# Hybrid diffusion layer: one 512-column matmul for the high and low activation parts, output blocks of 512 columns

## The chip, the cores and the metric

The kernel runs on one core of one Trainium2 chip. The metric is the device time of one execution in microseconds; the median of three runs of the kernel before is 2029.83 us (2029.54 to 2030.59).

## The reference

One layer of a backbone is applied to 128 context tokens and 128 latent tokens with the same weights, 2048 channels wide, all in float32. For each of the two rows of tokens:

```python
h = rmsnorm(x, norm1_g) * (1 + scale1) + shift1          # shift, scale, gate from silu(c) @ w_mod
parts = split(h @ w_in)                                  # 17440 columns
o_a = hgrn2_branch(...)                                  # gated linear recurrence, both directions
o_b = chunk_mlp_branch(...)                              # 128x128 mixing per channel group
o_c = gdn_branch(...)                                    # short conv, gated delta rule, both directions
merged = g_a * (o_a @ w_br_hg) + g_b * (o_b @ w_br_cm) + g_c * (o_c @ w_br_gdn)
x = x + gate1 * (merged @ w_out)
h2 = rmsnorm(x, norm2_g) * (1 + scale2) + shift2
x = x + gate2 * (square(relu(h2 @ w_ff1)) @ w_ff2)       # hidden width 8192
y = rmsnorm(x, final_g)
```

The outputs are y of both rows and the final states of the two recurrences of the context row.

## The kernel before

**The weight stream.** Activations lie channel-major, 128 channels on the partitions and 256 columns (128 context tokens, 128 latent tokens). Every weight matrix passes through SBUF once, in units of 128x1024 numbers (512 KB). ScalarE rounds a unit to float32r (`wh`, the high part) and VectorE subtracts (`wl`, the low part); `split` does it, three pairs of buffers ahead at most, and a split waits until TensorE has finished with the pair that it overwrites. The activations are split the same way into a high tile (`Hh`, `oah`, half of `hid`) and a low tile (`Hl`, `oal`, the other half). `block` multiplies: for each 128x128 weight block there are three matmuls with 256 moving columns each, high*high, low*high, high*low, all into the same 256 columns of PSUM:

```python
ops = ((hi[:, w], ah), (lo[:, w], ah), (hi[:, w], al))
```

I call these three a triple. The weight is the stationary operand and is loaded for each. A block is 1024 output columns (8 column tiles) wide; two column tiles share a PSUM bank of 512 numbers, so a block fills 4 of the 6 banks that the stream has. The loop goes over the k-tiles outside and the column tiles inside, so the first bank of a finished block is complete some 18 matmuls ahead of the last. When the block is done, `evac` empties its banks: one ScalarE or VectorE instruction per bank (activation function, product with a gate, residual, or copy). The next block starts in the two spare banks and then needs the first two banks of the block before.

Two blocks (`win(0)` and `win(10)`, orient "A") have it the other way around: the activations are stationary and 512 weight columns move. The last columns of `w_out` and `w_ff2` go in narrower blocks (`PIECES`).

**The fillers.** All mixer work (recurrences, conv, norms, the gMLP) is written as generators that `pump` interleaves with the stream's matmuls. A planner (`Clock`, `Meter`) computes when each engine gets to its instructions; `pump` adds filler stages while VectorE and ScalarE are at most `margin` (1.8 us) ahead of TensorE, and near a block's end at most `DVEE` = 2.0 us (VectorE) and `ACTE` = 0 (ScalarE) beyond the end that it expects. The planner takes 0.1093 us for a 256-column matmul. The lowest filler is the background, `mods`: it forms the modulation vectors gate1, shift2, scale2 and gate2 on VectorE (the tiles `junk<-mraw,cb`); `drain_mod` forces what is left of it where it is needed, ahead of `w_out` and of the second norm. `finish` emits all that is left of a filler, whatever TensorE has to wait for.

**One such place matters here.** `start_gmlp` (line 1498) starts the gMLP as a filler once its input `vBf` (slot 6) is there. The next block is `gate(1, 0, 6)`, whose result goes into slot 6 as well, so its `evac` first calls `self.finish(*self.before.values())` (line 1455): the gMLP must be done with `vB` by then. The gMLP consists of `head_rms`, four `part`s (two loads, four matmuls, three VectorE instructions each, with two scratch tiles between them, so two parts at a time) and four `parts` that split the result.

**Order of the stream.** Start (modulation columns, hff, half of hfb), hq, rest of hfb, hi, hgo, q, k, v, ggo, then gates and branch products in turn, `w_out`, second norm, and the MLP in four groups of 2048 hidden channels: `ff1` (relu, square, split) and `ff2` (partial sums in `Y`, at the end the residual `resid`).

Of the kernel before, what the change touches and what calls it, by code (L numbers as in the profile page):

```python
# [30 lines left out]
HEADS = 8  # L31
W = "wait"
# [9 lines left out]
class Clock:  # L42
    """A model of when every engine gets to its instructions: in order, each once the data and
    buffers that it names are free. The fillers are placed by it."""
# [11 lines left out]
    def place(self, tile, key, bufs):  # L56
        """A new tile in a pool's ring of buffers waits for the last use of the one before."""
# [34 lines left out]
    def book(self, e, reads, writes, cost, hop=0.0):  # L92
        """Start and end of an instruction of engine e."""
# [23 lines left out]
class Meter:  # L117
    """An engine whose instructions go into the clock."""
# [4 lines left out]
    def cost(self, name, a, k, out):  # L123
# [49 lines left out]
class Pool:  # L173
    """A tile pool whose tiles the clock knows."""
# [18 lines left out]
class Backbone:  # L193
    """Activations are channel-major ([channel, row*128 + token], row 0 the context, row 1 the
    latents). A weight matrix streams through SBUF once; each 128x128 block of it is the stationary
    operand of three float32r products (high*high, low*high, high*low), which together carry
    float32's mantissa."""
# [27 lines left out]
    def slot(self, z, shape, dt=F32):  # L225
# [7 lines left out]
        return v  # L233

# [47 lines left out]
    def grab(self):  # L282
        """A filler bank for work outside the fillers."""
# [33 lines left out]
    def step(self, g, forced=False):  # L317
        """One stage of a filler, once what its last stage did is ready; True if it did something."""
# [15 lines left out]
    def force(self, gens):  # L334
        """The stage that is ready first, of these fillers or else of any."""
# [6 lines left out]
    def finish(self, *gens):  # L342
        """Emit what is left of these fillers."""
# [6 lines left out]
    def together(self, *gens):  # L350
        """Runs generators side by side."""
# [5 lines left out]
    def now(self, gen):  # L357
        """Emit a generator at once; its value."""
# [8 lines left out]
    def rsqrt(self, v, n, tag, scale=None):  # L367
        """1/sqrt(v), with a Newton step after the square root and the reciprocal."""
# [13 lines left out]
    def split(self, hi, lo, x):  # L382
        """hi + lo == x exactly: hi rounds to float32r, lo is what is left."""
# [12 lines left out]
        # while the slots are empty they lend buffers to the start  # L396
# [53 lines left out]

    def block(self, units, nk, xh, xl, evac, orient="B", pre=None):
        """Steps of one block of output columns: NB columns a k-tile, or, where a unit holds two
        k-tiles, NB/2."""
# [4 lines left out]
        nb = 4 // per  # L458

        def do(u, hi, lo):  # L460
# [4 lines left out]
            if u >= len(units) - 2:  # L465
                self.evac = self.t["pe"] + 24 * 0.107 * (len(units) - u)
            for k in range(u * per, u * per + per):
                off = (k - u * per) * (NB // per)
                ah, al = xh(k), xl(k)
                for c in range(2 * nb if orient == "B" else nb):  # L470
                    if orient == "B":
                        o = st["b"][c // 2][:, (c % 2) * 256:(c % 2) * 256 + 256]
                        w = slice(off + c * P, off + c * P + P)
                        ops = ((hi[:, w], ah), (lo[:, w], ah), (hi[:, w], al))
                        first, lastc = c % 2 == 0, c % 2 == 1
                    else:
                        o = st["b"][c]
                        w = slice((c % 2) * 512, (c % 2) * 512 + 512)
                        t = slice((c // 2) * P, (c // 2) * P + P)
                        ops = ((ah[:, t], hi[:, w]), (ah[:, t], lo[:, w]), (al[:, t], hi[:, w]))  # L480
                        first = lastc = True
                    for j, (a, b) in enumerate(ops):
                        nc.tensor.matmul(o, lhsT=a, rhs=b, start=(k == 0 and j == 0 and first),
                                         stop=(k == nk - 1 and j == 2 and lastc), skip_group_check=True)
                    if lastc:
                        self.pump()
# [9 lines left out]
    def setup(self):  # L496
# [12 lines left out]
        # conditioning vectors: silu, then high and low parts as stationary columns  # L509
# [51 lines left out]
    def rstd(self, x, gain=None):  # L561
        """1/rms of every token, on all partitions, in a filler bank; the last two tiles go in here."""
# [25 lines left out]
    def modulate(self, which, n0, x, r, wait=True):  # L588
        """(x * r) * gs + shift for channel tiles n0, n0 + 1, split into the stream's operands."""
# [35 lines left out]
    def start_steps(self, first, second):  # L625
        """shift1 and scale1, 256 channels at a time, the input norm for those channels, and the
        products of the first blocks of input columns with them."""
# [11 lines left out]
        def bounds():  # L639
            # softmax over the one layer, minus its first entry  # L640
# [61 lines left out]
        for db in range(8):  # L702
            wins.append([dict(kind="call", do=lambda db=db: self.finish(self.chains[db])), first[2 * db]])
            wins += [[first[2 * db + 1]], [second[db]]]
# [1051 lines left out]
```

## Time and profile before

| | |
|---|---|
| median of three timed runs | 2029.83 us |
| span of the profiled execution | 2026.0 us |
| VectorE busy | 1492.9 us |
| ScalarE busy | 1016.9 us |
| mean granted TensorE clock | 0.994 |

The span runs from the first to the last instruction of the one profiled execution; the timed runs have 3.8 us more around it. All tensor instructions carry line 169, since one helper issues them, so groups are told apart by tiles: `pb` is a PSUM bank of the stream, `pf` one of the fillers, `z` any of the twelve slots, `wh` and `wl` the split weights. A row of the timeline gives the start, the length, the engine, the operation with out<-in, and how many instructions it merges; a start-to-start distance of neighbouring matmuls is what one costs, since their recorded lengths overlap. DVE is VectorE, ACT ScalarE, PE TensorE.

### The profile page before, as it was taken

The numbers are of one execution on the slowest core, as the hardware profiler recorded it, in microseconds if no ns is written. First come the engines' busy times: TensorE is split into PE (matmuls) and PEld (weight loads), VectorE is DVE, ScalarE is ACT, GpSimd is POOL, SyncE is SP. The second block draws the span as 40 slices with busy tenths as digits, with TensorE's granted clock in tenths as the row PEclk, the third lists the DMA queues.
The fourth block names the chain that finished last, engine by engine and source line by source line (L and its number), as shares of the span: only waits on it lengthen the run. The fifth ranks groups of instructions, "written<-read, shape, count | busy, mean of one in ns | idle before, by whom it ended". The sixth has DMA issues, their size and how long they took to land.

```text
span 2026.0 us, 39412 instructions
## 1 busy us (share of the span) xinstructions
PE 1980.4 (98%) x15829; PEld 1915.5 (95%) x15829; DVE 1492.9 (74%) x2662; ACT 1016.9 (50%) x1475; POOL 47.4 (2%) x117
## 2 busy tenths in 40 slices
PE   5999999999999999999999999899999999999997
PEld 3779989999999999899999999899999999999997
DVE  5886797967877997877888878588878554455565
ACT  6774645466645545365634434644444443344343
POOL 0000000000000001110000000000000000000000
PEclk9999999999999999999999999999999999999998
DMA  9887756665566767776778787577787555555654
GB/s 342 309 305 226 231 192 199 198 194 173 166 192 217 255 220 227 248 236 227 234 258 273 260 279 245 178 240 260 246 271 255 186 182 183 186 180 186 213 192 137
DMA packets 143055, 455.82 MB, mean 225 GB/s; under 512 B 16248, under 2 KB 16920, under 8 KB 141848
## 3 DMA queue, kind: packets, MB, share of 16 engines
q1 hardware_dynamic: 135216, 423.96, 63.4%
q0 software_dynamic: 7360, 29.07, 4.4%
q8 instruction: 124, 2.03, 0.4%
q14 instruction: 59, 0.48, 0.1%
q10 hardware_dynamic: 296, 0.27, 0.0%
HBM read 442.74 MB, written 10.50 MB: 224 GB/s over the span
## 4 chain that ended last, share of the span: by engine, by line
PE 90%; DVE 3%; DMA 3%; ACT 2%; issue 1%; SPq 0%; POOL 0%; DVEq 0%; ACTq 0%; POOLq 0%
PE pb L169 81%; PE pf L169 9%; DVE wl L169 1%; DVE z L169 1%; DVE m L169 1%; ACT wh L169 1%; DMA raw<-in_wmods 1%; DMA raw<-in_wouta 1%; DMA mraw<-in_wmodr 0%; DVE junk L169 0%; DMA z<-sp 0%; ACT tp L169 0%; DMA raw<-in_winh 0%; DMA raw<-in_win 0%; DMA z<-in_wmods 0%
## 5 line engine op out<-in xcount | busy, mean ns | idle before, releaser
L169 DVE TENSOR_TENSOR wl<-raw,wh 128x1024 fp32r<-128x1024 f32 x610 | 742.5, 1220 | 455.2 <-ACT wh L169 454.0
L169 ACT CAST wh<-raw 128x1024 fp32r<-128x1024 f32 x610 | 637.0, 1046 | 856.1 <-PE pb L169 745.2
L169 PE MATMUL pb<-Hh,wh 128*128 128x256 f32 x3144 | 898.5, 286 | 4.0 <-ACT Hh L169 2.6
L169 PE MATMUL pb<-Hl,wh 128*128 128x256 f32 x3144 | 890.5, 283 | 2.2 <-DVE Hl L169 2.2
L169 PE MATMUL pb<-Hh,wl 128*128 128x256 f32 x3144 | 890.3, 283 | 0.9 <-DVE wl L169 0.8
L169 PEld LDWEIGHTS pb<-Hh,wh 128*128 128x128 f32 x3144 | 602.4, 192 | 8.0 <-ACT Hh L169 3.0
L169 PEld LDWEIGHTS pb<-Hl,wh 128*128 128x128 f32 x3144 | 602.2, 192 | 3.1 <-DVE Hl L169 3.0
L169 PEld LDWEIGHTS pb<-Hh,wl 128*128 128x128 f32 x3144 | 602.5, 192 | 2.2 <-DVE wl L169 1.3
L169 PE MATMUL pb<-z,wh 128*128 128x256 f32 x2816 | 508.5, 283 | 0.0
L169 PEld LDWEIGHTS pb<-z,wh 128*128 128x128 f32 x2816 | 437.3, 190 | 0.2 <-DVE z L169 0.2
L169 PE MATMUL pb<-z,wl 128*128 128x256 f32 x1408 | 397.4, 282 | 0.0
L169 DVE SCALAR_TENSOR_TENSOR junk<-mraw,cb 128x512 bf16<-128x512 f32 x512 | 330.7, 685 | 16.4 <-DMA mraw<-in_wmodr 14.1
L169 PEld LDWEIGHTS pb<-z,wl 128*128 128x128 f32 x1408 | 268.2, 190 | 0.2
L169 DVE TENSOR_TENSOR z<-z,z 128x512 fp32r<-128x512 f32 (+2 forms) x76 | 59.1, 823 | 7.3 <-ACT z L169 7.2
L169 DVE SCALAR_TENSOR_TENSOR cy<-z,par,cy 128x258 f32<-128x258 f32 (+1 forms) x192 | 53.6, 331 | 1.9
L169 PE MATMUL pb<-wh,Hh 128*128 128x512 f32 x128 | 53.4, 417 | 0.0
L169 PE MATMUL pf<-m,z 128*128 128x128 f32 x384 | 50.5, 275 | 0.4 <-DVE m L169 0.4
L169 ACT ACTIVATE z<-pb 128x512 f32<-128x512 f32 x88 | 48.5, 600 | 3.5 <-PE pb L169 0.5
L169 PE MATMUL pb<-wh,Hl 128*128 128x512 f32 x128 | 50.1, 391 | 0.0
L169 PE MATMUL pb<-wl,Hh 128*128 128x512 f32 x128 | 50.0, 390 | 0.0
L169 PEld LDWEIGHTS pf<-m,z 128*128 128x128 f32 x384 | 47.6, 192 | 2.1 <-DVE m L169 1.0
L169 ACT CAST z<-z 128x512 fp32r<-128x512 f32 (+1 forms) x56 | 40.2, 771 | 17.7 <-PE pb L169 9.0
(171 smaller groups left out, 1323.2 us busy)
## 6 DMA issues: line engine op xcount, KB each, us to landing
raw<-in_win SPq DMA_DIRECT2D x249, 512.0 KB, 4.0
raw<-in_wff SPq DMA_DIRECT2D x224, 512.0 KB, 3.9
mraw<-in_wmodr SPq DMA_DIRECT2D x256, 256.0 KB, 4.2
raw<-in_wbr SPq DMA_DIRECT2D x48, 512.0 KB, 4.0
z<-in_wmods SPq DMA_DIRECT2D x39, 512.0 KB, 5.3
raw<-in_wmods SPq DMA_DIRECT2D x25, 512.0 KB, 5.7
cb<-csd POOLq DMA_DIRECT2D x16, 512.0 KB, 5.8
raw<-in_wouta SPq DMA_DIRECT2D x16, 512.0 KB, 5.0
```

What stands on the lines that cost most here:

```text
L169: return f(*a, **k)
```

## The change

High and low parts of the activations are put side by side: `H` is [128, 16, 2, 256], and the operands in slots come from `pairs`. The triple becomes a pair of matmuls ("wide"): the high weights times all 512 columns, high and low activations together, into a whole bank, then the low weights times the 256 high columns, into the bank's second half. The bank then holds high*low in its first half and the sum of the other two products in its second half; `gather` adds the halves when the bank is emptied: ScalarE copies the second half out, VectorE adds the first to it. A column tile now takes a whole bank, so a block is 512 output columns wide (4 banks as before), and each unit holds two k-tiles of 512 columns. The old form ("thin", three matmuls) stays for hff, the first half of hfb, the first two blocks of `ff1` and the last 512 columns of `w_out` and `w_ff2`; the orientation "tokens" is the old "A". The inner loop is now over a unit's two k-tiles, with the column tiles outside it.

With it go: an activation function is applied in a separate instruction after `gather`; branch products are gathered into a new tile `ev` before the gate multiplies them; in `ff1` relu and square become one VectorE instruction; `resid` and the sums into `Y` read both halves, with twice the instructions per number of columns; gates call `finish` at the evacuation of their first 512 columns; the planner takes 0.120 us for 256 columns and 0.227 us for 512; `dynamic_dma_scratch_size` is set to 8192. Comments go.

```diff
-            return max(n * 4.27e-4, 0.107) if k["rhs"].dtype == F32R else max(n * 1.7e-3, 0.214)
+            return n * 4.17e-4 + 0.0133 if k["rhs"].dtype == F32R else max(n * 1.7e-3, 0.214)
...
+        cost = {"wide": 0.347 * nt, "thin": 0.36 * nt, "tokens": 0.341 * nt}[orient] * per
...
-            for k in range(u * per, u * per + per):
-                for c in range(2 * nb if orient == "B" else nb):
-                        ops = ((hi[:, w], ah), (lo[:, w], ah), (hi[:, w], al))
+            for c in range(nb if orient == "tokens" else nt):
+                for k in range(u * per, u * per + per):
+                    pair = x(k)
+                    ah, al = pair[:, 0, :], pair[:, 1, :]
+                    if orient == "wide":
+                        b = st["b"][c]
+                        ops = ((b, hi[:, w], pair.rearrange("p a b -> p (a b)")), (b[:, 256:512], lo[:, w], ah))
...
+    def gather(self, outs, b):
+        for o, x in zip(outs, b):
+            self.nc.scalar.copy(o, x[:, 256:512])
+        for o, x in zip(outs, b):
+            self.nc.vector.tensor_tensor(out=o, in0=x[:, 0:256], in1=o, op=ALU.add)
...
-        self.Hh = self.sp.tile([P, 16, 256], F32R, tag="Hh", name=self.nm("Hh"))
-        self.Hl = self.sp.tile([P, 16, 256], F32R, tag="Hl", name=self.nm("Hl"))
+        self.H = self.sp.tile([P, 16, 2, 256], F32R, tag="H", name=self.nm("H"))
+        self.Hh, self.Hl = self.H[:, :, 0, :], self.H[:, :, 1, :]
...
+                self.gather([t[:, n0 + c, :] for c in range(4)], b)
+                for j in range(2):
+                    v = flat(t, n0 // 2 + j)
+                    nc.scalar.activation(v, v, func)
...
-            return win(11 + 2 * i + half, evac=lambda b: (self.finish(*self.before.values()), e(b)))
+            def evac(b, n0):
+                if n0 == 0:
+                    self.finish(*self.before.values())
+                e(b, n0)
+            return sum(win(f"gate{2 * i + half}", evac), [])
...
+                e = self.sp.tile([P, 1024], F32, tag="ev", name=self.nm("ev"))
+                self.gather([e[:, c * 256:c * 256 + 256] for c in range(4)], b)
+                nc.vector.tensor_tensor(out=g, in0=e, in1=g, op=ALU.mult)
...
-        PIECES = (("a", 0, 0), ("b", 0, 8), ("c", 0, 12), ("c", 1, 14))
+        PIECES = (("a", 0, 0), ("a", 1, 4), ("a", 2, 8), ("c", 0, 12), ("c", 1, 14))
+        form = lambda n0: "wide" if n0 < 12 else "thin"
...
+                    parts = ((b[j], 0), (b[j], 256)) if wide else ((b[j // 2], (j % 2) * 256),)
+                    for x, c in parts:
+                        nc.vector.scalar_tensor_tensor(out=o, in0=x[:, c + s * P:c + s * P + P], ...)
...
-                    nc.vector.tensor_tensor(out=r[:, j, :], in0=r[:, j, :], in1=r[:, j, :], op=ALU.mult)
+                    nc.vector.scalar_tensor_tensor(out=v, in0=v, scalar=0.0, in1=v, op0=ALU.max, op1=ALU.mult)
...
+                for h in (0, 256):
+                    for o, x in zip(y, b):
+                        nc.vector.tensor_tensor(out=o, in0=x[:, h:h + 256], in1=o, op=ALU.add)
```

More of the change, by code (lines that the diff above doesn't have):

```diff
@@ L31 @@
 HEADS = 8
+WIN = ("hff", "hfb", "hq", "hgo", "q", "k", "v", "ggo", "cu", *(f"gate{j}" for j in range(6)))
 W = "wait"
@@ L233, in slot, with pairs, halves @@
         return v
+    def pairs(self, *zs):
+        return [self.slot(z, [P, 4, 2, 256], F32R) for z in zs]
+    @staticmethod
+    def halves(pairs, n):
+        t = pairs[n // 4]
+        return t[:, n % 4:n % 4 + 2, 0, :], t[:, n % 4:n % 4 + 2, 1, :]
     def mid(self, z, shape, dt=F32):
@@ L479, in do @@
                         t = slice((c // 2) * P, (c // 2) * P + P)
[L480 to L486, printed above, removed]
+                        ops = ((b, ah[:, t], hi[:, w]), (b, ah[:, t], lo[:, w]), (b, al[:, t], hi[:, w]))
@@ L487, in do @@
+                    for j, (o, l, r) in enumerate(ops):
+                        nc.tensor.matmul(o, lhsT=l, rhs=r, start=(k == 0 and j == 0 and first),
+                                         stop=(k == nk - 1 and j == len(ops) - 1), skip_group_check=True)
+                self.pump()
             if u == len(units) - 1:
@@ L623, in make_gs, with start_steps @@
                                        op0=ALU.add, op1=ALU.mult)
-    def start_steps(self, first, second):
+    def start_steps(self, blocks):
         nc = self.nc
@@ L1462, in evac, with branch @@
+        def branch(i, half, operand, order, pre=None):
+            def evac(b, n0):
+                g = four(getattr(self, f"gate{i}{half}"), n0)
                 if order == 0:
-                    if half == 0:
-                        self.merged = [None, None]
-                    self.merged[half] = self.slot(1 + half, [P, 8, 256])
-                if order == 2 and half == 0:
-                    self.newH()
-                for j in range(4):
-                    m = flat(self.merged[half] if order == 0 else g, j)
-                    nc.vector.tensor_tensor(out=m, in0=b[j], in1=flat(g, j), op=ALU.mult)
@@ L1471, in evac @@
-                if order > 0:
-                    self.before[i, half] = self.brgen[i, half] = self.add(tail(g), first=True)
-            def tail(g):
-                for j in range(4):
-                    m = flat(self.merged[half], j)
-                    nc.vector.tensor_tensor(out=m, in0=m, in1=flat(g, j), op=ALU.add)
+                    if n0 == 0:
+                        if half == 0:
+                            self.merged = [None, None]
+                        self.merged[half] = self.slot(1 + half, [P, 8, 256])
@@ L1478, in tail @@
+                nc.vector.tensor_tensor(out=g, in0=e, in1=g, op=ALU.mult)
+                self.before[i, half, n0] = self.brgen[i, half, n0] = self.add(tail(g, n0), first=True)
+            def tail(g, n0):
+                m = four(self.merged[half], n0)
+                for j in range(2):
+                    c = slice(512 * j, 512 * j + 512)
+                    nc.vector.tensor_tensor(out=m[:, c], in0=m[:, c], in1=g[:, c], op=ALU.add)
                 if order < 2:
@@ L1565, in run, with ff1 @@
         self.hid, self.hidgen = {}, {}
-        def ff1(g, blk):
+        def ff1(g, blk, orient="wide"):
             def pre():
@@ L1572, in pre @@
                     z = (8, 9, 10, 11) if g % 2 == 0 else (0, 1, 2, 3)
[L1573 removed]
+                    self.hid[g] = self.pairs(*z)
             def square(r):
[L1576 to L1578 removed]
+                parts = [self.halves(self.hid[g], 4 * blk + 2 * j) for j in range(2)]
@@ L1600, in ff1 @@
-            return steps
+                r = self.slot(4 if blk % 2 == 0 else 7, [P, 4, 256])
+                if orient == "thin":
+                    for j in range(2):
+                        nc.scalar.copy(flat(r, j), b[j])
+                else:
+                    self.gather([r[:, c, :] for c in range(4)], b)
+                self.hidgen[g, blk] = self.add(square(r), first=True)
+            return self.block([I["wff1"][4 * g + blk, k] for k in range(8)], 16, hx, evac, orient=orient, pre=pre)
@@ L1602, in ff2, with ff1_first @@
+        def ff1_first():
+            a, b = ff1(0, 0, "thin"), ff1(0, 1, "thin")
+            out = []
+            for k in range(8):
+                out += call(lambda k=k: norm2(k)) + [a[k], b[k]]
+            return out
         def ff2(g, part):
-            c, i, n0 = PIECES[part]
+            c, i, n0 = PIECES[part] if g == 3 else ("", 0, 4 * part)
             def evac(b):
```

255 lines of the change are left out of this document (128 added, 127 removed).

## The prediction

> **What bounds the kernel now.** I read the page first, for the engine that is never idle.
>
> ```profile
> span 2026.0 us, 39412 instructions
> ...
> PE 1980.4 (98%) x15829; PEld 1915.5 (95%) x15829; DVE 1492.9 (74%) x2662; ACT 1016.9 (50%) x1475; POOL 47.4 (2%) x117
> ...
> PE 90%; DVE 3%; DMA 3%; ACT 2%; issue 1%; SPq 0%; POOL 0%; DVEq 0%; ACTq 0%; POOLq 0%
> ```
>
> TensorE is busy for 98% of the span and makes up 90% of the chain that ended last; nothing else is near. So a change pays exactly what it takes off TensorE's instruction stream, less what it makes TensorE wait. The next question is what a matmul costs there. Recorded lengths overlap, so I count starts: in the timeline of a calm stretch for 256 columns, and of a block of the other orientation for 512.
>
> ```profile
> 1699.80 0.28 PE L169 MATMUL pb<-z,wl 128*128 128x256 f32 x1
> ...
> 1702.68 0.28 PE L169 MATMUL pb<-z,wl 128*128 128x256 f32 x1
> 1700.00:1750.00 50.00, 50.00 (x419) 50.00 (x418) 24.17 (x22) 17.80 (x17) 0.00 (x0) 1.00 0.57 186
> 246.34 0.39 PE L169 MATMUL pb<-wh,Hl 128*128 128x512 f32 x1
> ...
> 249.74 0.39 PE L169 MATMUL pb<-wh,Hl 128*128 128x512 f32 x1
> ```
>
> Eight triples lie between the first two rows: 2.88 us / 24 = 120.0 ns a matmul. The window row (busy time and count of PE, PEld, DVE, ACT, POOL; granted clock 1.00) gives 50 / 419 = 119.3 ns. Fifteen matmuls of 512 columns take 3.40 us, 226.7 ns each. Twice the columns therefore cost 12 to 13 ns less than twice the time: about 13 ns of every matmul do not depend on its columns.
>
> **What the change takes away.** The columns streamed stay the same (3 x 256 = 512 + 256). A triple is 3 x 119.7 = 359 ns, the pair that replaces it 226.7 + 119.7 = 346.4 ns. That is 12.6 ns saved; with 119.3 it is 11.9, with 120.0 it is 13.3. How many triples: q-to-gate names 15 x 128, branches 384, `w_out` 256, `ff1` 1024, `ff2` 1024, together 4608. Thin stay three blocks at the start (192), two of `ff1` (128) and the last columns of `w_out` and `w_ff2` (64 + 64), so 4160 change. 4160 x 12.6 ns = **52.4 us** (49.5 to 55.3). Weight loads fall from three to two; they lie beside the matmuls, as the equal 13 ns at both widths shows, so I give them no price of their own.
>
> The Trainium skill (TensorE: Matmul & The Clock Gate, "Back-to-back issue gap") gives the warm distance as N/2.4 + 2.5 ns; by it a pair would save 2.5 ns and the change 10.4 us. The rows above do not agree: 119.7 and 226.7 ns lie 13 ns over N/2.4, so here the measured 13 ns decide.
>
> **What emptying the banks adds.** For a bank of one column tile there is now a ScalarE copy of 256 and a VectorE add of 256. The nearest rows, from the groups by form and the timeline:
>
> ```profile
> L169 ACT COPY z<-pb 128x256 f32<-128x256 f32 x24 | 7.1, 400 | 0.1
> 1261.01 0.43 DVE L169 TENSOR_TENSOR m<-m 128x256 f32<-128x256 f32 x1
> 1688.36 1.23 DVE L169 TENSOR_TENSOR wl<-raw,wh 128x1024 fp32r<-128x1024 f32 x1 [1.65 <-ACT wh L169]
> 1689.50 2.48 DVE L169 TENSOR_TENSOR z<-pb,z 128x512 f32<-128x512 f32 x4
> 225.00:1250.00 1025.00, 1020.19 (x8167) 998.80 (x8166) 845.23 (x1722) 531.14 (x887) 40.63 (x101) 1.00 0.68 224
> ```
>
> 71 blocks become wide: 27 of input columns, 12 of branches, 3 of `w_out`, 14 of `ff1`, 15 of `ff2`. Four adds are at most 4 x 0.43 = 1.7 us of VectorE a block, about 120 us in all with the product in `ev` and the doubled residual instructions; ScalarE gets about as many copies and loses the `ff1` Relus. VectorE goes to some 1613 us of 1990, 81%. From 225 to 1250 us, where the fillers are, it is idle for 1025 - 845 = 180 us, and about 75 us of the new work falls there. So the work has room; what counts is when a bank is free.
>
> A block's first bank is complete 2.1 us before the block ends (three column tiles of 0.69 us are still to come); the next block needs it 1.4 us after the end (two column tiles in the spare banks). Between them lie a copy (0.40) and an add (0.43). In the rows above VectorE was held by a weight split up to the block's end, and would then still free the bank 0.4 us later, a full 1 us early. It gets late only where a filler is in front. The trace has that case, at branch blocks, which VectorE empties already:
>
> ```profile
> 738.72 1.56 DVE L169 TENSOR_TENSOR m<-m,m 128x192 f32<-128x192 f32 x4
> 740.20 2.48 DVE L169 TENSOR_TENSOR z<-pb,z 128x512 f32<-128x512 f32 x4
> PE pb L169 <- DVE z L169: 1.4, 2, 1.1
> ```
>
> The block had ended at about 738.1; recurrence work kept VectorE for 2 us more, and TensorE waited: 1.4 us over two such blocks (1.8 us by starts) of the three that lie among recurrence fillers, none at the five later ones. That is 0.6 us a block; the first add is 0.2 us shorter than the 512-column product of now, so 0.4. Among recurrence fillers lie 27 of the new wide blocks: 27 x 0.4 = **11 us** lost; ends 0 (VectorE always in time) and 27 x 1.25 = 34 us (each like the worse of the two). The 8 `ff2` blocks of groups 1 and 2 add both halves of all banks in two rounds, so the first bank needs five adds: 5 x 0.35 = 1.75 us from 0.2 us before the end, 0.3 us late with the hop: 8 x 0.3 = **2.4 us** (0 to 5).
>
> **What moves: `finish` at gate(1,0).** The gMLP had a whole block of 1024 columns to run beside; now it must be done at the first 512.
>
> ```profile
> 862.00:895.50 33.50, 24.78 (x191) 23.25 (x191) 0.00 (x0) 0.73 (x2) 1.00 0.72 229
> 890.57 1.28 ACT L169 ACTIVATE z<-z,rshd 128x128 f32<-128x128 f32 x4
> 890.76 0.54 POOL L169 DMA_DIRECT2D tp<-in_bs  x1
> 908.17 0.54 POOL L169 DMA_DIRECT2D tp<-in_bs  x1
> 918.74 0.69 DVE L169 TENSOR_TENSOR z<-z,z 128x512 f32<-128x512 f32 x1
> 927.43 1.28 DVE L169 TENSOR_TENSOR z<-z,z 128x512 fp32r<-128x512 f32 x2
> 930.10 2.06 ACT L169 ACTIVATE z<-pb 128x512 f32<-128x512 f32 x4
> ```
>
> The first row is of `pb` alone: 191 of the block's 384 matmuls are done by 895.5. At that point `head_rms` has just ended (891.9), the loads of two `part`s are issued and those of the other two are not; the gMLP ends at 928.7, right when the gate is emptied at 930.1. Cut at the half, 33 us of its course are left, to be forced. Compressed: two parts to 898, the scratch tiles free, loads and matmuls of the other two to about 905, the splits of the result to 909, then the gate can leave its banks. TensorE has 1.4 us in the spare banks and some 3 us of recurrence matmuls in it: 13.5 - 4.4, **10 us** of standing with a cold start behind it. Ends: 0, if the gMLP is by then through, and 33 us.
>
> What a stand costs afterwards shows at the second norm:
>
> ```profile
> 1273.32 0.58 PE L169 MATMUL pb<-Hh,wh 128*128 128x256 f32 x1 [2.58 <-ACT Hh L169]
> 1273.69 0.41 PE L169 MATMUL pb<-Hh,wl 128*128 128x256 f32 x1
> ...
> 1277.41 0.36 PE L169 MATMUL pb<-Hl,wh 128*128 128x256 f32 x1
> ```
>
> Sixteen distances in 3.72 us are 232 ns each, so 1.8 us are lost before 120 ns returns; I count it within the 10. The skill's same page ("The HAM clock gate") says that an idle window of about 3.4 us halves the clock until a busy one has passed, which agrees.
>
> **Cover that stays.** The recurrences' results have slack (last gating products, then the matmuls that first need them):
>
> ```profile
> 533.48 0.75 DVE L169 SCALAR_TENSOR_TENSOR tp<-pf,par,z 128x512 f32<-128x512 f32 x1
> L169 PE MATMUL pb<-z,wh x2816: 274/283/469, 631.0 to 2011.7; 128*128 128x256 f32 x188
> 999.96 0.74 DVE L169 SCALAR_TENSOR_TENSOR tp<-pf,par,z 128x512 f32<-128x512 f32 x1
> 1126.78 0.28 PE L169 MATMUL pb<-z,wh 128*128 128x256 f32 x1
> 1256.27 0.19 DVE L169 TENSOR_TENSOR modc<-part,modc 128x32 f32<-128x32 f32 x1
> 1268.08 0.18 DVE L169 SCALAR_TENSOR_TENSOR gs<-modc,par 128x32 f32<-128x32 f32 x1
> ```
>
> They have 97 and 127 us; 75 us of added VectorE work, spread over both, doesn't use that up. The background has little: scale2 is ready at 1256.3 and wanted at 1268.1. The planner's slower (truer) 256-column matmul lets it place some 50 us more filler work up to there, the adds take 60 to 75. I take **2 us** of forced draining, between 0 and 13 (ten tiles of 1.3 us, two products of 0.6 us each).
>
> **The sum.** -52.4 + 11 + 2.4 + 10 + 2 = -27 us. The profiled execution has a span of 2026.0, so 1999 for the new one; the timed median is 3.8 us (0.19%) above that span, for what lies around it, which the change does not touch. 2029.8 - 27 = **2003 us**.
>
> **Rivals.**
> 1. *Everything stays hidden*: the adds find VectorE free and the gMLP is through or costs a few us. For it: the slack of 1 us at calm blocks, and no evacuation stall after 1000 us in the trace. Against: the two stalls above. 2029.8 - 52.4 = 1977, up to 1990.
> 2. *VectorE becomes the bound at the block ends.* Each wide block waits for it, twice as many ends as now. The point from which it decides: (52.4 - 12) / 71 = 0.57 us of mean wait a block. The price of the worse case seen is 1.25 us; at 1.0 us on all 71 it gives 2029.8 - 52.4 + 71 + 12 = 2060, slower. For it: the planner lets VectorE run 2 us past a block's end, and its old, too short matmul times hid that; against: in the last third there are no fillers.
> 3. *The pair costs what the triple did*, the 512-column matmul twice 119.7 ns when the weights are stationary, so that nothing is saved and only the 25.4 us of losses are left: 2029.8 + 25.4 = 2055. Against it are the 226.7 ns, taken with activations stationary and weights moving. (The skill's 2.5 ns per matmul, section as above, would give 10.4 us of saving and 2045; the rows speak against it as much.)
> 4. *The losses come out twice as large*: near 2030.
>
> **How the numbers follow.** Forecast (1990 to 2022) 0.62; rival 1 0.2; rival 2 0.06; rival 3 0.03; rival 4 0.09, of which two thirds lie within 0.2% (about what a measurement of this kernel can tell from no change). Faster 0.62 + 0.2 + 0.03 = 0.85, same 0.06, slower 0.09. The range runs from rival 1's 1977 to 2026, the forecast with the gMLP and the banks at twice their price.
>
> **What would show it.** Right: starts of a wide pair 346 ns apart; VectorE near 80%; a stand of about 10 us in `pf` and `pb` a half block after `vBf`; short waits of `pb` for VectorE's slots between 225 and 1000 us. Wrong: pairs at 359 ns; no stand at gate(1,0); waits of 1 us at most block ends; a stand ahead of the second norm that is longer than now.

## The result, and the profile after

The changed kernel takes **2063.35 us** (2061.29 to 2065.61, four runs), the kernel before 2029.68 beside it: a ratio of 1.0169, interval 1.0155 to 1.0184. It is slower by 34 us, where 27 us of gain were predicted, and outside the range of 1977 to 2026.

The head and the busy times of the page after, then its waits of TensorE (line waited for: us in total, times, longest):

```profile
span 2061.7 us, 31687 instructions
...
PE 1970.2 (96%) x11653; PEld 1701.9 (83%) x11653; DVE 1591.8 (77%) x2999; ACT 1074.2 (52%) x1668; POOL 47.5 (2%) x117
```

```profile
PE pb L171 <- DVE z L171: 23.5, 28, 3.6
PE pf L171 <- DVE m L171: 15.7, 6, 11.0
PE pf L171 <- ACT wh L171: 15.4, 1, 15.4
PE pb L171 <- ACT H L171: 7.7, 3, 3.0
PE pb L171 <- DVE ev L171: 4.6, 5, 2.5
...
PE pf L171 <- DMA tp<-in_wsT: 2.2, 1, 2.2
```

The span is 35.7 us longer, although TensorE has 4176 instructions fewer to do. (The medians differ by 33.7 us. In every run of the changed kernel and of the experiments the timed execution is 1.8 us longer than its own span. So of the 3.8 us that the prediction put around the span some 2 are probably only that the profiled execution of the kernel before was quicker than the median.) The first row of waits was 1.4 us in two cases before, the second 3.3 us with a longest of 1.3; the third was 15.9 us, is the start, and has hardly moved.

To see both sides of the account I took every distance from one matmul's start to the next in both traces and split it into the steady pitch of its kind and what is more than 60 ns over it:

| sum over the trace, us | before | after |
|---|---|---|
| 4160 k-tile products, as triples / as pairs | 359.1 ns each | 351.3 ns each (234.3 + 117.0) |
| over the pitch, weight stream | 29.5 | 84.5 |
| over the pitch, filler matmuls | 25.5 | 39.8 |

The pairs save 4160 x 7.8 ns = 32.6 us. The stands grow by 69 us. The difference, 36.7, is the 35.7 us of the span to within what the records resolve. So there are two questions: why the pair saves 7.8 ns and not 12.6, and where 69 us of stands come from. By what ended them, some 32 of the 69 us are late block ends, and some 12 are waits for `DVE m`, the second norm above all. Another 12 to 13 us are lost by matmuls that run at half the granted clock, mostly behind a stand. The rest is spread over smaller waits.

One late block end, from the timeline after (VectorE and TensorE rows; the last figure of a row in brackets is the idle time ahead of it and its releaser):

```profile
696.30 1.23 DVE L171 TENSOR_TENSOR wl<-raw,wh 128x1024 fp32r<-128x1024 f32 x1
...
697.45 0.69 DVE L171 SCALAR_TENSOR_TENSOR junk<-mraw,cb 128x512 bf16<-128x512 f32 x1
...
698.06 0.69 DVE L171 SCALAR_TENSOR_TENSOR junk<-mraw,cb 128x512 bf16<-128x512 f32 x1
...
698.67 0.69 DVE L171 TENSOR_TENSOR z<-z,tri 128x512 f32<-128x512 f32 x1
699.39 0.69 DVE L171 TENSOR_TENSOR z<-z,gB 128x512 f32<-128x512 f32 x1
700.00 1.41 DVE L171 TENSOR_TENSOR z<-pb,z 128x256 f32<-128x256 f32 x4
700.47 0.49 PE L171 MATMUL pb<-H,wh 128*128 128x512 f32 x1 [2.71 <-DVE z L171]
```

The four adds that free the banks (700.00) stand behind a split, two background products (`junk`) and two products of a recurrence. TensorE has used up its two spare banks and stands for 2.71 us until the first add is through. By starts 35 of the 71 wide block ends are late, by 0.97 us on the mean, 33.9 us together; before the change it was 1.8 us.

The second norm, the rows of both traces at which TensorE gets the scale of the tokens, and the background product that this scale waits for (after):

```profile
1270.03 0.71 PE L169 MATMUL pf<-ident,m 128*128 128x128 f32 x4 [1.27 <-DVE m L169]
```

```profile
1305.79 0.69 DVE L171 SCALAR_TENSOR_TENSOR junk<-mraw,cb 128x512 bf16<-128x512 f32 x1 [3.84 <-DMA mraw<-in_wmodr]
...
1308.36 0.19 DVE L171 TENSOR_TENSOR modc<-part,modc 128x32 f32<-128x32 f32 x1
...
1309.92 1.22 PE L171 MATMUL pf<-ident,m 128*128 128x128 f32 x4 [11.01 <-DVE m L171]
```

The background's last sum for scale2 was ready at 1256.3 before, 12 us early; now it is ready at 1308.4, and TensorE stands for 11 us for it. VectorE doesn't work through all of these 11 us: for 3.84 of them (the first row) it waits for a load of the background, which the kernel issues only two tiles ahead. Up to TensorE's row the changed kernel is 39.9 us behind. From there to the span's end it takes 751.8 us against 756.0. **All of the loss lies ahead of the second norm; behind it the change gains 4 us.**

### The profile page after: what moved, and what is told of

Its sections match the earlier page's. It is cut to its first block, busy times and chain, and to the rows that moved or that the text cites. A ratio compares the mean times of both kernels' runs of the same rounds, so it can differ in the third digit from the quotient of the medians.

```text
span 2061.7 us, 31687 instructions
## 1 busy us (share of the span) xinstructions
PE 1970.2 (96%) x11653; PEld 1701.9 (83%) x11653; DVE 1591.8 (77%) x2999; ACT 1074.2 (52%) x1668; POOL 47.5 (2%) x117
## 5 line engine op out<-in xcount | busy, mean ns | idle before, releaser
L171 PE MATMUL pb<-H,wh 128*128 128x512 f32 (+1 forms) x3456 | 1135.6, 382 | 24.1 <-DVE z L171 16.0
L171 PE MATMUL pb<-H,wl 128*128 128x256 f32 x3144 | 885.8, 282 | 2.6 <-DVE wl L171 2.6
L171 PEld LDWEIGHTS pb<-H,wh 128*128 128x128 f32 x3456 | 635.8, 190 | 161.9 <-DVE z L171 18.3
L171 PEld LDWEIGHTS pb<-H,wl 128*128 128x128 f32 x3144 | 598.1, 190 | 3.6 <-DVE wl L171 2.8
L171 PE MATMUL pb<-z,wh 128*128 128x512 f32 (+1 forms) x1472 | 500.8, 389 | 10.7 <-DVE z L171 7.3
L171 PEld LDWEIGHTS pb<-z,wh 128*128 128x128 f32 x1472 | 273.1, 189 | 74.8 <-DVE z L171 7.2
L171 ACT COPY z<-pb 128x256 f32<-128x256 f32 (+3 forms) x225 | 73.6, 356 | 45.9 <-PE pb L171 44.0
L171 DVE TENSOR_TENSOR z<-pb,z 128x256 f32<-128x256 f32 (+1 forms) x285 | 93.9, 391 | 2.2 <-ACT z L171 1.7
L171 PE MATMUL pb<-wh,H 128*128 128x512 f32 x256 | 89.7, 405 | 0.0
L171 DVE TENSOR_TENSOR z<-z,z 128x512 fp32r<-128x512 f32 (+3 forms) x80 | 64.8, 845 | 8.9 <-ACT z L171 8.3
```

The costliest lines, as they stand in the source:

```text
L171: return f(*a, **k)
```

## The experiments

**The planner's line alone.** The change also gives the planner truer durations. In the kernel before, only that line:

```diff
-            return max(n * 4.27e-4, 0.107) if k["rhs"].dtype == F32R else max(n * 1.7e-3, 0.214)
+            return n * 4.17e-4 + 0.0133 if k["rhs"].dtype == F32R else max(n * 1.7e-3, 0.214)
```

> The kernel before, with one line of the new one: the planner takes 0.120 and 0.227 us for 256 and 512 columns in place of 0.109 and 0.219. Nothing else changes, no instruction is added. Theory A (the exact planner packs VectorE fuller, so that it gets late at block ends and norms): 2040 to 2050 us, with waits of the stream's banks for VectorE above the 1.4 us of before. Theory B (the planner is harmless and the wide form itself costs the time): 2024 to 2034 us.

2044.98 us (2042.99 to 2046.12), ratio 1.0076 (1.0052 to 1.0100). The line alone costs the old kernel 15 us. Its window from 550 to 800 us (columns: busy time and count of PE, PEld, DVE, ACT, POOL; clock, DMA share, GB/s), ahead of it that of the kernel before:

```profile
550.00:800.00 250.00, 248.21 (x1994) 242.32 (x1993) 210.20 (x471) 127.27 (x213) 9.95 (x17) 1.00 0.66 218
```

```profile
550.00:800.00 250.00, 243.68 (x1980) 238.52 (x1980) 220.54 (x520) 123.76 (x215) 14.57 (x30) 0.99 0.68 224
```

With a slower TensorE in its books the planner puts 49 more VectorE instructions into this stretch, and TensorE is busy for 4.5 us less. Over the whole trace TensorE's waits for VectorE's `z` in `pb` rise only from 1.4 to 4.4 us, those for ScalarE's `z` from nothing to 2.9, and the distances at half clock from 5.1 to 11.6 us. So the time is as theory A had it, and late bank ends are only a part of it.

**The planner's old durations in the changed kernel**, the same line turned back:

> The changed kernel with the planner's matmul times of before (256 columns 0.109, 512 columns 0.219 us). Theory A: VectorE gets 6% less filler work per unit, bank waits for VectorE fall from 28 us (z and ev) to under 12, time 2035 to 2048. Theory B: bank waits stay above 20 us, time within 8 us of 2063; the second norm may wait longer, as the background gets less room.

2085.06 us (2082.73 to 2087.39), ratio 1.0274. Not faster but 22 us slower, which neither theory had. Its waits:

```profile
PE pf L171 <- DVE m L171: 58.7, 3, 56.2
...
PE pb L171 <- DVE z L171: 14.0, 17, 2.3
```

The late block ends are nearly halved, and TensorE stands 56 us ahead of the second norm for the background.

**No fillers in front of the adds:** `DVEE = -1.0`, so the planner stops VectorE's fillers 1 us ahead of a block's end.

> The changed kernel with DVEE = -1.0 in place of 2.0: no filler is put on VectorE once its planned time is within 1 us of the block's end. Theory C' (filler work queued ahead of the adds makes them late): bank waits for VectorE fall from 28 us to under 8, and as cold starts go too the time is 2030 to 2045. Rival (the chain copy, add, hop is too long even with a free VectorE): waits stay above 20 us and the time at 2055 or more. The background loses room, so the wait ahead of the second norm may grow by up to 10 us.

2081.43 us (2080.85 to 2082.00), ratio 1.0256.

```profile
PE pf L171 <- DVE m L171: 75.1, 3, 73.6
...
PE pb L171 <- DVE z L171: 2.1, 5, 0.8
```

The block ends are cured, as the theory said, and the stream comes to `w_ff1` 9 us earlier than in the kernel before (its first load at 1245.9 against 1255.0). But the time it gives was wrong: the work that no longer stands ahead of the adds is owed at the second norm, in one stand of 73.6 us, where up to 10 us more had been expected.

**Half of the background**, on top of that (each row's product over half of its columns, the other half left out):

```diff
-                nc.vector.scalar_tensor_tensor(out=junk[:, v], in0=w, scalar=1.0, in1=cb[:, :, v, :],
+                nc.vector.scalar_tensor_tensor(out=junk[:, v, 0:2], in0=w[:, 0:2], scalar=1.0, in1=cb[:, 0:2, v, :],
```

> e4 (no fillers near a block's end) with half of the background's VectorE work: each product runs over 256 of its 512 numbers, so the modulation vectors gate1, shift2, scale2 and gate2 are summed over half of their rows. Theory E (before the second norm VectorE has not enough time for the background beside the adds; what is not drained there shows as bank waits): the wait ahead of the second norm falls from 74 us to under 8, bank waits stay under 4, time 2000 to 2015. Rival (the wait at the second norm is the planner's doing, whatever the amount of work): the wait stays above 30 us, time above 2040.

2035.79 us (2033.84 to 2036.82): 45.6 us less, and the stand ahead of the second norm falls from 73.6 to 21.6 us. So the time follows the background's work ahead of that point, but the expectation (under 8 us, 2000 to 2015) was missed. What VectorE waits for in that stand, from 1263.0 to 1284.6 us:

```profile
DVE junk L171 <- DMA mraw<-in_wmodr: 10.0, 9, 5.5
```

It is busy for 11.1 of the 21.6 us and waits for the background's loads for 10.0. So such a stand is a price of late work and of late loads together; a run that loads further ahead was not made.

**No adds.** The changed kernel without `gather`'s VectorE add (nor that of q, k, v):

```diff
-        for o, x in zip(outs, b):
-            self.nc.vector.tensor_tensor(out=o, in0=x[:, 0:256], in1=o, op=ALU.add)
```

> The changed kernel without the VectorE adds of the bank halves (in gather and for q, k, v): only the half with high*high and low*high is copied out, the high*low half is left out of those sums. A bank is free after the ScalarE copy. Theory C (the added VectorE step in the release of a bank, and its 105 us of work, cost what was lost): bank waits for VectorE fall to under 5 us, the second norm's wait for the background to under 4 us, time 2005 to 2020. Theory D (the matmul pair itself is dearer than worked out, by its pitch of 351 in place of 346 ns): the pitch stays at 351 ns, and of 2063 at most 10 us go.

2029.67 us (2024.99 to 2036.69, eight runs), ratio 1.0007 (0.9992 to 1.0022). The adds cost 34 us. That is more than the 10 us of theory D and less than theory C had. Even without them the wide kernel is no faster than the old one, though its pairs save some 30 us. Its trace (of the slowest of the eight executions) has some 40 us more of stands than the trace before; 12 of them are half clock (17.7 against 5.1 us), none behind the start is longer than 3.5 us, and what causes them was not tested.

**No adds and the old durations**, to see whether the two losses, 34 and 15 us, add up:

> The changed kernel with the VectorE adds left out (high*low is left out of the result) and with the planner durations of the kernel before. If the two losses add up, 2029.7 - 15 = 2015 us (2008 to 2022). If the old durations help only where they keep VectorE from running ahead (the wide kernel with them alone was slower, 2085), the background comes late here too: a stand ahead of the second norm of 10 us or more, 2025 to 2050 us.

2050.44 us (2048.38 to 2056.99), ratio 1.0107. They don't. With the old durations and no adds the stand ahead of the second norm is there again:

```profile
PE pf L171 <- DVE m L171: 45.4, 3, 43.8
```

So the adds are not all that makes the background late, and neither planner fits the wide kernel: with the true durations VectorE's fillers stand in front of what TensorE needs, with the short ones the background comes late. Why it does so even without the adds was not settled; the next reading bears on it.

**Is VectorE's idle time room?** The prediction had counted 1025 - 845 = 180 us of idle VectorE from 225 to 1250 us. The waits of VectorE in that stretch, before and after:

```profile
DVE wl L169 <- ACT wh L169: 152.1, 136, 4.5
DVE junk L169 <- DMA mraw<-in_wmodr: 13.0, 18, 2.0
```

```profile
DVE wl L171 <- ACT wh L171: 128.4, 96, 4.7
```

Nearly all of it, 152 of 180 us, ends at a split's subtraction. It waits for ScalarE's copy, which waits for TensorE to be done with the pair of buffers; and if VectorE takes its queue in order, what is queued behind it waits as well. To tell whether that time can be used, the subtraction was put into the queue 0.7 us of the planner's TensorE time behind the copy, in both kernels (the next weight load is issued with it, so that moves too):

```diff
-            self.split(hi, lo, w)
-            hl[n] = (hi, lo, p, max(t["act"], t["dve"]) + READY)
+            nc.scalar.copy(hi, w)
+            hl[n] = (hi, lo, p, t["act"] + 1.5 + READY)
+            def rest():
+                self.later = None
+                nc.vector.tensor_tensor(out=lo, in0=w, in1=hi.bitcast(F32), op=ALU.subtract)
...
+            self.later = (t["pe"] + 0.7, rest)
```

> The changed kernel, but a split's subtraction is put into VectorE's queue 0.7 us of the planner's TensorE time behind the ScalarE copy that it needs, so that filler work can stand ahead of it. Theory (VectorE's idle time is no room: its queue is held at the head by a subtraction that waits for the copy, and the work behind it waits too): VectorE's wait for wh between 225 and 1245 us, 128.4 us, falls below 90, the background is further on at 1245 us, and the time falls by 8 to 25 us, to 2038 to 2055. Rival (the wait at the split only shows that VectorE is ahead and nothing is queued): the wait falls, but the background and the time stay, 2058 to 2068, or weights come late and it is slower.

> The same edit in the kernel before. There the background is in time by 12 us and stalls ahead of the second norm are few, so by the theory little is to be had: 2022 to 2032 us, with the wait for wh (152.1 us in that stretch) lower and the background ready earlier than 1256 us. By the rival the background's time does not move.

The changed kernel comes to 2050.83 us (2048.90 to 2051.57), 12.5 less than without the edit (ratios 1.0110 against 1.0169, intervals 1.0093 to 1.0127 and 1.0155 to 1.0184). The kernel before stays at 2028.21 (ratio 1.0001). From the changed kernel with the late subtraction, first VectorE's wait in that stretch, then the waits of TensorE:

```profile
DVE wl L172 <- ACT wh L172: 100.7, 75, 3.2
```

```profile
PE pb L172 <- DVE z L172: 25.5, 26, 3.2
...
PE pf L172 <- DVE m L172: 2.5, 2, 1.3
```

The wait for `wh` fell by 28 us (less than the 38 expected), and VectorE is busy for 885.4 us of the stretch instead of 868.5. The background's products (`junk`) done in it are 360, all that the kernel lets run ahead of the second norm; the changed kernel had done 330 and the old one 355. The stand for the second norm is gone, and the 12.5 us are about what it cost; the late block ends are not gone. In the old kernel the background also comes earlier (1216 instead of 1256 us), and nobody waits for it; with no more of it to do, the wait for `wh` stays at 147.7 of 152.1 us. So some of the idle time, 17 of 156 us in the changed kernel, was blocked by the order of VectorE's queue, and where the background is late, freeing it pays. That the rest could be freed is not shown.

**The gMLP's place.** `vBf` before `uB`, so that the gMLP starts 44 us earlier ahead of gate(1,0). Only `head_rms` can use them, since the `part`s now wait until `uB` is there (a flag that is not shown here):

```diff
-        steps += sum(win("cu", act_evac("uB", 5, AF.Gelu)), [])
         steps += tok(1, "vBf", 6, AF.Gelu)
...
+        steps += sum(win("cu", act_evac("uB", 5, AF.Gelu)), [])
```

> The changed kernel with the block for vBf ahead of the two blocks for uB, so that the gMLP has those 44 us more before gate(1,0) calls finish. Theory H (the forced gMLP costs what was worked out, some 10 us): the waits of TensorE in the 25 us around the first evacuation of gate(1,0), 10 us with the cold starts, go, and the time is 2051 to 2056. Rival (VectorE has to do the same work before the second norm anyway, so that the wait only moves there): 2060 to 2066, with a longer wait ahead of the second norm.

Two timed runs, 2049.28 and 2065.61 us: too far apart to put a price on it. In the trace (of the faster one) the two longest stands at gate(1,0) are gone, 1.92 and 0.82 us remain there, and ahead of the second norm stands one of 13.0 us, 2 longer than in the changed kernel.

**The low product into the first half of the bank** (`b[:, 0:256]` instead of `b[:, 256:512]`), and **two wide, then two narrow products** for the two k-tiles of a column tile:

> The changed kernel with the low-weight product accumulated into the first half of the bank in place of the second; the sum of both halves is the same. Theory F (adding to columns that the 512-column matmul wrote last holds the pair up): the mean start distance in the calm stretch of 250 us of the last third falls from 235 + 117 = 352 ns a pair to about 347, time 2040 to 2046. Rival: 352 ns stay, time 2058 to 2067.

> The changed kernel with a unit's two 512-column matmuls of a column tile behind each other, then its two 256-column ones. Theory G (a change of width costs about 5.5 ns, as 227 and 120 ns hold among equals): four matmuls take 699 ns in place of 704, time 11 us less, 2048 to 2056. Rival (a 512-column matmul with the weights stationary always takes 235 ns): 704 ns or more stay, time 2058 to 2067.

One run each: 2058.1 and 2066.7 us. In the first a pair still takes some 351 ns on the mean of the trace, so theory F is not borne out. The pitch of the second fell to 348.5 ns a pair, as theory G had it, but not the time: behind the second norm it gains 5 us on the changed kernel, while ahead of it TensorE arrives 3 us later (1302.1 against 1298.9) and the background is ready 8.5 us later (1316.9), a stand of 16.3 us (`DVE m` 20.3 in all). So the faster pitch doesn't show where VectorE's work is owed; with one run, how it got lost there stays open.

**The pair's price by itself.** Products alone, eleven stretches of 512 k-tiles, from one resident weight tile and one resident activation tile:

> The products alone: eleven stretches of 512 k-tiles each from one resident weight tile and one resident activation tile, and nothing else of the layer (its outputs are the last bank). In order: triples; wide pairs; wide pairs from another activation tile; only the 512-column products; only the 256-column products; wide pairs beside a busy VectorE, beside a busy ScalarE, beside a busy DMA, beside all three; triples beside all three; wide pairs alone again. The prediction's term was a pair at 346.4 ns against a triple at 359; the kernels ran pairs at 351.3 on the mean. Theory (the pair's own pitch is 346 and what runs beside it slows it): pairs 344 to 348 in the quiet stretches, 351 to 356 in one or more of the loaded ones, triples 353 to 360. Rival (the 512 columns cost 5 to 10 ns more when the narrow product stands between them, whatever runs beside): pairs 350 to 356 in the quiet stretches too, while the 512-column products alone take 227 each and the narrow ones 120.

Windows of that run, in order: triples; pairs; pairs from the other tile; 512-column products only; pairs beside VectorE; pairs beside all three.

```profile
60.00:160.00 100.00, 100.00 (x836) 100.00 (x835) 0.00 (x0) 0.00 (x0) 0.00 (x0) 1.00 0.00 1
250.00:350.00 100.00, 100.00 (x568) 86.71 (x568) 0.00 (x0) 0.00 (x0) 0.00 (x0) 1.00 0.00 1
400.00:500.00 100.00, 100.00 (x568) 86.77 (x567) 0.00 (x0) 0.00 (x0) 0.00 (x0) 1.00 0.00 1
580.00:660.00 80.00, 80.00 (x355) 66.26 (x354) 0.00 (x0) 0.00 (x0) 0.00 (x0) 1.00 0.00 1
...
770.00:900.00 130.00, 130.00 (x738) 112.67 (x737) 123.90 (x180) 0.00 (x0) 0.00 (x0) 1.00 0.00 1
...
1330.00:1440.00 110.00, 110.00 (x624) 95.33 (x623) 104.82 (x153) 104.68 (x169) 0.00 (x0) 1.00 0.61 211
```

Two or three matmuls in each count only reach into the window from ahead of it. By starts a triple takes 360.0 ns, a 512-column product among its like 226.7, a 256-column one 120.0, and a pair 353.3 to 353.4 (236.0 to 236.8 and 116.6 to 117.4), in every loaded stretch as in the quiet ones. So the two pitches don't add up to the pair's: in turn, the two products cost 6.6 ns more than their sum of 346.7. And neither VectorE, ScalarE nor the DMA has a part in it. The rival was right about the numbers.

Order and place of the operands, again the products alone:

> The products alone again, in eleven stretches of 448 k-tiles, nothing beside them (the rest of the layer is left out). In the run before a pair took 353.4 ns whatever ran beside it; in the kernels whole blocks ran at 346 to 354. In order: pairs into one bank; pairs over four banks; the same, two k-tiles to a bank as in the kernel; two 512 then two 256, one bank; the same over four banks; eight and eight; sixteen and sixteen; pairs with weights at another place; pairs with activations at another place; triples with these; the kernel's order with both. Theory (each change between a wide and a narrow product costs some 3 ns): 353 for all pairs in turn, 350 in twos, 347.5 in eights, 347 in sixteens, whatever the place. Rival (the place of the operands in memory sets it, as the blocks of the kernels suggest): pairs at another place take 346 to 350 and their triples under 360, and the order changes nothing.

By starts, per k-tile: pairs in turn 351.1, over four banks 351.1; two and two 348.3; eight and eight 351.3; sixteen and sixteen 351.4; weights at another place 353.3; activations at another place 353.3, and the triple there 353.3, not 360.0 as in the run before; two and two with both at another place, under the kernel's order, 350.7. Neither account holds whole: the order matters by 3 ns in twos and not in sixteens, and the place by 2 ns for pairs. Sixteen and sixteen hardly change size any more and still take 351.4, so the change of size alone is not the cause. What sets it stays open. For the account it is enough that no stretch of pairs ran at 346.4 ns here; in the kernels single blocks come near it.

**Wide pairs where VectorE has time.** If the loss lies ahead of the second norm, the kernel before should be kept up to there, and the wide form used behind it: the second half of `ff1`'s first group, its other groups, and `ff2` but for its last group (26 blocks), with the true durations and `DVEE = -1.0` from there on:

```diff
+            if k["rhs"].dtype == F32R:
+                return n * 4.17e-4 + 0.0133 if self.clock.mlp else max(n * 4.27e-4, 0.107)
...
+        steps += call(lambda: setattr(self.clock, "mlp", True)) + ff1_first() + call(lambda: setattr(self, "late", True)) + ...
```

> The kernel before up to the second norm (1024-column blocks of triples, its planner durations); wide pairs, 512-column blocks and the exact planner durations only behind it, for ff1 behind its first two blocks and for ff2 but for its last group: 26 blocks of 64 pairs. No filler goes in front of an evacuation there (DVEE -1.0). Theory (the change loses ahead of the second norm, where VectorE has the recurrences, the adds and the background to do before one fixed point; behind it only one chunk of the background is left): the second norm comes when it came in the kernel before (its broadcast near 1270), and the stretch from there to the last matmul, 746.9 us before and 737.1 in the run with the fillers stopped, takes 735 to 742: 2018 to 2025 us. Rival (the wide form gives its gain back wherever it stands, by its adds and its pitch): the stretch takes 745 to 752, 2028 to 2035 us.

> The same kernel, but the planner keeps the durations of the kernel before and lets fillers in front of an evacuation as before (DVEE 2.0) behind the second norm too. If late adds still cost there, 3 to 6 us more than the kernel that stops the fillers: 2021 to 2031 us; if the adds find VectorE free behind the second norm, the same time within 2 us.

2015.08 us (2011.87 to 2015.88, five runs), ratio 0.9928 (0.9915 to 0.9942): faster than both kernels, and 3 us below the range expected. With the old planner and fillers in front of the evacuations there, 2017.69, ratio 0.9946 (0.9933 to 0.9958), between its two expectations: late adds cost little behind the second norm. And with the two k-tiles of a column tile in twos:

```diff
+                for _, _, o, l, r, s0, s1 in sorted(todo, key=lambda q: q[0]):
+                    nc.tensor.matmul(o, lhsT=l, rhs=r, start=s0, stop=s1, skip_group_check=True)
```

> The kernel with wide pairs in the MLP only, and in each unit the two wide products of a column tile ahead of its two narrow ones. If the order of the products sets the pitch (348.3 against 351 to 353 ns alone), 1664 pairs save 3 to 5 ns each: 5 to 8 us under that kernel's 2015.1, 2007 to 2010. If the place of the operands or something else sets it, the time stays at 2013 to 2016.

**2007.69 us** (2006.76 to 2009.76), ratio 0.9901 (0.9886 to 0.9915). The row of the second norm in these two kernels, each with its page's span ahead of it:

```profile
span 2011.3 us, 36263 instructions
...
1266.41 1.23 PE L173 MATMUL pf<-ident,m 128*128 128x128 f32 x4 [1.28 <-DVE m L173]
```

```profile
span 2005.3 us, 36265 instructions
...
1266.62 0.71 PE L173 MATMUL pf<-ident,m 128*128 128x128 f32 x4 [1.27 <-DVE m L173]
```

From that row to the end: 756.0 us before, 744.9 wide, 738.7 wide in twos. (The row itself comes some 3.5 us earlier than in the trace before; 2 to 3 of these are already there at the background's first sum, at 243 to 246 us, ahead of all that differs in work, so I don't count them as a gain.) The late block ends there are down to nearly nothing. By starts the 1664 pairs of the second kernel sum up to 579.8 us instead of 584.6; a pair takes 348.3 to 349.0 ns in all of its stretches, as it did alone in twos, where the first kernel had 353.4 in some blocks and 346.8 in others.

## Why the prediction was wrong

- **TensorE bounds the kernel.** True for the kernel before, and the reason why the change looked good. A second bound was near: the background, ready 12 us early. The prediction saw these 12 us and gave them a price of 2.
- **The pair at 346.4 ns.** The step that failed is "226.7 + 119.7": two pitches, each measured among its own kind, added up. Together they took 351.3 ns in the kernel and 348.3 to 353.4 alone; why stays open. The saving was 32.6 us, not 52.4; 20 of the 60 us between forecast and result are this.
- **"So the work has room."** The second step that failed, and the larger one. 180 us of idle VectorE were set against 75 us of new work ahead of the second norm. 152 of them ended at a split's subtraction at the head of VectorE's queue, which the waits of VectorE said before the change; they weren't read. The adds found too little room: without them the time falls by 34 us, with half of the background by 46 (fillers stopped in both), and with the subtraction moved back, which let 17 us more of work into that stretch, by 12.5. The work that doesn't fit is paid at the block ends or at the second norm, wherever the planner leaves it.
- **The block ends, 11 us (0 to 34) and 2.4 for `ff2`.** The mechanism was right, the size was not: 35 ends late by 0.97 us, 33.9 us by starts, the far end of the term (1.8 of them were there before, and one end of 3.8 is the stand at gate(1,0) below). "In the last third there are no fillers" was wrong too: ten late ends lie behind the second norm, where the last chunk of the background still runs, though they cost only 5.5 us.
- **gate(1,0), 10 us.** Right in kind and about in size: stands at 925.3, 928.7 (2.23 us, for a load of the gMLP, as foretold) and 940.5 (3.60), some 7 us, and some 3 us of slow restart. (The prediction's own working gives 13.5 - 4.4 = 9.1 us; it took 10.)
- **The background, 2 us (0 to 13).** It took 12.4 us more (15.7 against 3.3), near the end given. The adds, which were the reason given, are only a part of it: with the old durations the stand is 43.8 us even without them.
- **The planner, at no price.** The prediction let its truer durations make room for 50 us of fillers and thought that a help. In the kernel before the same line costs 15 us. In the wide kernel it helps by 22 us: there it brings the background in time, and that outweighs what it costs elsewhere. No single price stands for both.
- **The rivals.** The one that came nearest is the second, VectorE as the bound at the block ends, with 2060 us. Its point of decision, a mean of 0.57 us a block, was not reached (33.9 / 71 = 0.48); with the true saving of 32.6 us and the 12 us of other losses the point lies at 0.29. What it lacked is that the block ends and the second norm are one account: the old durations and the stopped fillers, which helped the block ends, came back as stands at the second norm.

Not tried: a wide kernel in which the adds are done elsewhere than on VectorE, and a background spread otherwise.

## What to carry to other kernels

Before idle time of an engine is called room, read what ends it: if it is a queued instruction's own input, the time may not be open to what is queued behind it. Don't add up pitches that were measured in runs of one shape; measure the mix. And where a saving on one engine is bought with work on another, look for the next fixed point at which both must meet, and use the saving behind it first: here 26 blocks in the new form behind it gave 13 us, and 71 blocks on both sides of it cost 34.

## What had not been expected of the hardware

- With nothing beside it and a granted clock of 1.00, a triple of 256-column float32r products took 360.0 ns in one run of the products alone and 353.3 in the other, with its activations at another place; that the place makes the difference is likely, but no one run has both. A pair took 348.3 to 353.4 ns by place and order.
- A short stand can leave a slow clock behind. The matmuls after the stand at 700.47 shown above, and the window around it:

```profile
701.27 0.47 PE L171 MATMUL pb<-H,wh 128*128 128x512 f32 x1
701.54 0.42 PE L171 MATMUL pb<-H,wl 128*128 128x256 f32 x1
701.76 0.63 PE L171 MATMUL pb<-H,wh 128*128 128x512 f32 x1
702.19 0.41 PE L171 MATMUL pb<-H,wl 128*128 128x256 f32 x1
...
704.75 0.34 PE L171 MATMUL pb<-H,wl 128*128 128x256 f32 x1
```

```profile
700.00:750.00 50.00, 46.68 (x253) 39.95 (x254) 43.43 (x87) 23.99 (x37) 1.66 (x3) 0.97 0.57 186
```

One us after the stand the distances double (0.43 us for 512 columns, 0.21 for 256) and stay so for 3.2 us; the granted clock of the window is 0.97, where it was 1.00 before the change. Such stretches cost 17.7 us in all, against 5.1 before (distances more than 60 ns over their pitch, at half clock and without a wait in them): such a stand is paid in part a second time. The Trainium skill (TensorE: Matmul & The Clock Gate, "The HAM clock gate") has the clock fall after an idle window of about 3.4 us; here it fell after 2.71 us.
